# Decode state updates on row tiles of 32: two sequences in one product, two heads in two banks

## The chip, the cores and the metric

The kernel runs on one NeuronCore of a Trainium2 chip. The metric is the device time of one execution in microseconds (us); smaller is better. The engines are named as the profile names them: PE is the matrix engine and PEld its weight loads, DVE the vector engine, ACT the scalar engine, POOL the GpSimd engine, SP the engine that issues nearly all DMAs.

## What is computed

One decoder layer for 1024 prompt tokens and 8 decode sequences of 4 new tokens each (32 tokens). Two groups of four heads mix the tokens: an mLSTM (group a) and an HGRN2 (group b). Then come an output projection and a SwiGLU feed-forward layer. What matters here is the recurrent state of the decode sequences: each of the 8 sequences has a 128 x 128 matrix per head and group.

```python
# mLSTM, for each head:  num = w_inter * (q @ C) + (s_qk @ v)
C_new = decay[..., None, None] * C + jnp.einsum('bhs,bhsk,bhsv->bhkv', w_last, k, v)
n_new = decay[..., None] * n + jnp.einsum('bhs,bhsk->bhk', w_last, k)
...
# HGRN2, for each head:  inter = (q * exp(b)) @ S
S_new = jnp.exp(bL[:, :, 0, :])[..., None] * S + jnp.einsum('bhsk,bhsv->bhkv', k * jnp.exp(bL - b), v)
```

For a decode sequence the sums over s have four terms. The old state is needed twice: it is multiplied with the queries, and it is decayed and added to the new outer products.

## The kernel before

**Units and hooks.** The program is a list of units. A unit (`emit_k`, from L124) is one 128-row weight tile times a block of tokens: eight steps of the contraction, in each of them three products (L135 high weights by high activations, L136, L137), all into one PSUM bank of the tag `mm`. After every second step, and after the unit's evacuation, `hook()` (L63) is called: four hooks in a unit. Everything else is written as Python generators in a list `active`. A hook lets each of them write out its next instructions, in the order in which they were started; `yield n` means "go on n hooks later". So a hook is a place in the program order of all engines. Each engine works through its own instructions strictly in that order. `finish(key)` calls hooks until a generator is done, with no unit products in between.

**The token mixers.** The units come in the order: four heads of group a, each for three blocks of tokens (288, 384 and 384 wide, block 0 holding the 32 decode tokens), then four heads of group b in the same way. For group a the units of a block are q, k, v, o. The evacuation of a q or k unit (`conv_evac`, L404) writes out at once a chain of convolution steps on DVE (L435 to L445), a tanh on ACT (L449) and a last DVE step (L450). The prompt's mixing is `mix_a` (L506) and `mix_b` (L745), which take one to three banks of the tag `mx` at a time. There are four `mx` banks.

**The decode sequences.** `sample_a` (L700) and `sample_b` (L899) both go through `sample_core` (L600). The four heads' 32 tokens each lie on the 128 partitions: head h on partitions 32h to 32h+31.

- The keys are transposed (L612) and scaled into `ktm` (L619 to L624): a tile of [128, 4, 128] in which head h's block has its keys on its own 32 partitions and zeros elsewhere. The zeros come from a POOL memset in the first `mix_a` (L536). The values go to `vt` (L618).
- `prep(s)` (L628) makes for sequence s the queries with the other sequences' columns zeroed (`qz`, POOL) and the values with the other sequences' rows zeroed (`vm`, one DVE instruction, L634). In group a it also copies n into column 128 of the state tile.
- The loop over s (L667) multiplies queries with the old state: four products, one for each head, on column tiles of 32 (L672), into one bank `so` in which all sequences are summed.
- `update(s, vm)` (L639): four products `ktm[:, h, :]` by `vm`, each with the full 128 rows, into two `mx` banks (L644); one hook later four DVE instructions decay and add (L649), then the state is stored (L650).
- The state tiles `st` (L606) have two buffers, and `fetch(s + 2)` stands behind the store of s.

In group a the update of s directly follows its query products, and `prep(s + 1)` stands ahead of both; a sequence takes four hooks. In group b the loop does only the query products, every two hooks; a second generator `updates()` (L654), started at its end, fetches the states again and updates them, seven hooks for each sequence, with three hooks between `vm` (L660) and the products.

**Float32 products** appear in the trace as two passes: one `matmul` call with plain float32 operands gives two LDWEIGHTS and two MATMUL rows, so that the 32 calls of L644 in a group show as 64 rows. The unit products use a one-pass type and show one row each.

**What the driver forces.** `finish(("sa",))` stands four units into group b (L1791), `start(sample_b())` at the unit 12 x 3 + 8 of group b (L1793), and `finish(("su",))`, which waits for `updates()`, in the feed-forward part (L1816).

Of the kernel before, what the change touches and what calls it, by code (L numbers as in the profile page):

```python
# [24 lines left out]
H = 4  # L25
# [3 lines left out]
NS = 5  # L29
# [11 lines left out]
def hybrid_step(ctx: ExitStack, tc: tile.TileContext, i, o):  # L41
# [156 lines left out]
    def norm_rstd(key, n, acc, w=(2, 3)):  # L198
        """the rstd of n tokens on all partitions, from the squares summed over the feature tiles in acc"""
# [18 lines left out]
    def norm_gen(key, x, hv, lv, acc, vg, w=(2, 3), pb=None, lo_dve=(0, 4), step=2):  # L218
        """x = hv + lv = x * rstd * g, rstd from the squares summed over the feature tiles in acc"""
# [17 lines left out]
    # ------------------------------------------------------------------ token mixers  # L237
# [3 lines left out]
    # per-feature constants  # L241
# [26 lines left out]
    # ---- mLSTM gates  # L268
# [127 lines left out]
    # ---- mLSTM  # L396
# [57 lines left out]
    def early(name, h, b):  # L454
        if (name, h, b) == ("v", 0, 0):
            return ktm.rearrange("p h t -> p (h t)")
        if name != "q" or h or b == 2:
            return None
        return mp.tile([128, 4, 130], F32, tag="st", name="st", bufs=2).rearrange("p a c -> p (a c)")
# [30 lines left out]
    def norm_cols(s, sqs, nch, d2=None, p=128):  # L490
        """s = (sqs / 128 + EPS * d2) ** -0.5"""
# [14 lines left out]
    def mix_a(h, b):  # L506
# [28 lines left out]
        if (h, b) == (0, 0):  # L535
            nc.gpsimd.memset(ktm, 0.0)  # L536
# [63 lines left out]
    def sample_core(h_off, w, vnorm, st_in, decay, out_state, n_io, d2, k_scale, later=None):  # L600
        """the decode sequences of one head group: four heads x 32 tokens on the partitions"""
# [3 lines left out]
        def fetch(s):  # L605
            st = mp.tile([128, 4, 130], F32, tag="st", name="st", bufs=2)  # L606
            sts[s] = st
            nc.sync.dma_start(st[:, :, 0:128], st_in[s].rearrange("h k v -> k h v"))
        fetch(0)
        fetch(1)  # L610
# [8 lines left out]
        for h in range(H):  # L619
            hs = slice(32 * h, 32 * h + 32)  # L620
            if k_scale is None:
                nc.vector.tensor_copy(ktm[hs, h, :], pK[hs, 0:128])
            else:
                nc.vector.tensor_scalar_mul(ktm[hs, h, :], pK[hs, 0:128], k_scale[hs])  # L624
        pO = bank("so")
        vms, qzs = {}, {}

        def prep(s):  # L628
            st = sts[s]
            vm = vms[s] = mp.tile([128, 130], F32, tag="svm", name="svm", bufs=2)  # L630
            qz = qzs[s] = mp.tile([128, 4, 32], F32, tag="qz", name="qz", bufs=2)
            nc.gpsimd.memset(qz, 0.0)
            nc.gpsimd.tensor_copy(qz[:, :, 4 * s:4 * s + 4], qS[:, :, 4 * s:4 * s + 4])
            nc.vector.tensor_scalar_mul(vm[:, 0:w], vt[:, 0:w], seqm[:, s:s + 1])  # L634
            if w == 129:
                nc.gpsimd.tensor_copy(st[:, :, 128:129], n_io[0][:, 4 * s:4 * s + 4, None])
        prep(0)
        yield 3
        def update(s, vm):  # L639
            st = sts[s]  # L640
            pUs = [bank(), bank()]
            for h in range(H):
                u0 = (h % 2) * 130
                nc.tensor.matmul(pUs[h // 2][:, u0:u0 + w], ktm[:, h, :], vm[:, 0:w], start=True, stop=True)  # L644
            yield 1
            for h in range(H):
                u0 = (h % 2) * 130
                x = st[:, h, 0:w]
                nc.vector.scalar_tensor_tensor(x, x, decay(h, s), pUs[h // 2][:, u0:u0 + w], op0=OP.mult, op1=OP.add)  # L649
            nc.sync.dma_start(out_state[s].rearrange("h k v -> k h v"), st[:, :, 0:128])  # L650
            if w == 129:
                nc.gpsimd.tensor_copy(n_io[1][:, 4 * s:4 * s + 4, None], st[:, :, 128:129])

        def updates():  # L654
            fetch(0)
            fetch(1)
            yield 2
            for s in range(SEQS):
                vm = mp.tile([128, 130], F32, tag="svm", name="svm", bufs=2)
                nc.vector.tensor_scalar_mul(vm[:, 0:w], vt[:, 0:w], seqm[:, s:s + 1])  # L660
                yield 3
                yield from update(s, vm)
                if s + 2 < SEQS:
                    fetch(s + 2)
                yield 3

        for s in range(SEQS):  # L667
            if s + 1 < SEQS:
                prep(s + 1)
            st, qz = sts[s], qzs[s]  # L670
            for h in range(H):
                nc.tensor.matmul(pO[32 * h:32 * h + 32, 0:w], qz[:, h, :], st[:, h, 0:w], start=(s == 0), stop=False,  # L672
                                 skip_group_check=True, tile_position=(0, 32 * h))
# [54 lines left out]
    # ---- HGRN2  # L728
# [16 lines left out]
    def mix_b(h, b):  # L745
# [4 lines left out]
        samp = b == 0  # L750
        gx = tl("wib", 388, 2)
# [27 lines left out]
        while lv < 128:  # L779
# [123 lines left out]
    # ------------------------------------------------------------------ unit list  # L903
# [37 lines left out]
    # output projection; the token order from here on: 1024 prompt tokens, 32 decode tokens  # L941
# [62 lines left out]
    # feed-forward, first NPLAIN feature tiles  # L1004
# [36 lines left out]
    # feed-forward, the other feature tiles: pairs of them (rows of A) times two halves of the tokens (columns of B), the  # L1041
    # contraction in two halves: the seven products of Strassen and Winograd
# [21 lines left out]
    def t_prep():  # L1064
        """T1 = B12 - B11, T2 = B22 - T1, T3 = B22 - B12, T4 = B21 - T2"""
# [71 lines left out]
    def gsplit(g, u, dve=False):  # L1137
        """the factors of the products: A11 A12 | S1 = A21 + A22, S2 = S1 - A11 | S3 = A11 - A21, A22 | S4 = A12 - S2"""
# [52 lines left out]
    def g_out(u, r, th, j, ps, other=None, op=None):  # L1191
        """row tile r, token half th, columns j: ps or ps + other is there"""
# [54 lines left out]
    # down projection: NS times four feature tiles in the same way (the contraction in two pairs of tiles, pairs of output  # L1247
    # tiles, halves of the tokens), the last two tiles plainly
# [3 lines left out]
    def memb(r):  # L1252
        """place r of the ring of operands: hi and lo of two feature tiles, half of the tokens"""
# [18 lines left out]
    def raw_ff(c, f):  # L1272
        """the two column blocks of a feature tile: halves of the tokens, in the last chunk halves of each half"""
# [16 lines left out]
    def stage1(c):  # L1290
        """B11, T1 = B12 - B11, T2 = B22 - T1, B21"""
# [26 lines left out]
    def diffs(c, k):  # L1318
        """T3 = B22 - B12, T4 = B21 - B11 - T3"""
# [7 lines left out]
    def stage2(c):  # L1327
        """B22, T3, T4"""
# [28 lines left out]
    def dsplit(g):  # L1357
        """A11 A12 A22 | S1 = A21 + A22, S2 = S1 - A11, S4 = A12 - S2, S3 = A11 - A21"""
# [5 lines left out]
        def pair(j):  # L1364
            # the weights of the last chunk stay: five tiles in the ring, three in free places of the other ring
# [49 lines left out]
    def d_step(g, p):  # L1415
        """a product for a pair of output tiles, halves of the tokens; in the last chunk for two pairs, the quarters of a half"""
# [27 lines left out]
    # the first NPLAIN feature tiles of the down projection plainly  # L1444
# [36 lines left out]
    # the final norm: the first half of the tokens, then two quarters  # L1481
# [432 lines left out]
```

## Time and profile before

| | us |
|---|---|
| median of 3 runs | 1456.2 |
| lowest and highest run | 1451.91, 1456.57 |
| span of the profiled execution | 1451.2 |
| PE busy in it | 1376.6 |
| DVE busy in it | 904.0 |

The span is the time from the first to the last instruction of one profiled execution; it lies 5.0 us below the median of the runs and 0.7 us below the lowest of them. Rows of the timeline begin with the start and the duration in us; "x8" says that eight instructions were merged into the row, and brackets tell how long the engine had been idle and which instruction ended that. A matmul's start is recorded, its end is modelled, so the distance between starts is the safer measure of what a matmul costs.

### The profile page before, as it was taken

To read this page: it belongs to the slowest core of one execution; us is meant where nothing else is said; L and a number is where in the kernel's file an instruction comes from. 1 tells how busy PE (TensorE), PEld (TensorE's weight loads), DVE (VectorE), ACT (ScalarE), POOL (GpSimd) and SP (SyncE) were. 2 spreads that over 40 slices of the span, in tenths; PEclk is the share of its full clock that TensorE was granted. 3 is DMA by queue.
4 is the path that set the end of the run, shared out by engine and by line. 5 is a ranking of instruction groups with operands and counts; after the bars stand their busy time and mean duration, and the time that the engine had idled before them with its cause. 6 is when DMAs were issued, how large, how long until landed. Compare 5 with 4: busy or idle time off the path is not lost. (4 is left out here: it accounts for less than half of the span.)

```text
span 1451.2 us, 26916 instructions
## 1 busy us (share of the span) xinstructions
PE 1376.6 (95%) x10384; PEld 1339.6 (92%) x10384; DVE 904.0 (62%) x2120; ACT 528.8 (36%) x1195; POOL 731.9 (50%) x720
## 2 busy tenths in 40 slices
PE   7879999999999999999989999999999999998886
PEld 7769999999999998899989999999999998888885
DVE  7876657666776767745472233233322389999986
ACT  6554433322222223223344343333334423333343
POOL 5313213234343435223456655656555778888854
PEclk9989999999999999999999999999999999999998
DMA  6012212320010114443542222222212563334303
GB/s 216 22 42 76 64 37 86 109 79 29 33 44 18 44 32 133 142 148 119 182 139 74 82 89 89 69 72 89 89 64 69 182 235 134 134 134 145 123 30 121
DMA packets 85833, 138.54 MB, mean 95 GB/s; under 512 B 8240, under 2 KB 61000, under 8 KB 85192
## 3 DMA queue, kind: packets, MB, share of 16 engines
q1 hardware_dynamic: 85272, 136.57, 28.7%
q8 instruction: 82, 1.34, 0.4%
q14 instruction: 47, 0.39, 0.1%
q10 hardware_dynamic: 432, 0.24, 0.1%
HBM read 107.03 MB, written 29.75 MB: 94 GB/s over the span
## 5 line engine op out<-in xcount | busy, mean ns | idle before, releaser
L135 PE MATMUL mm<-HI,whi 128*128 128x384 f32 (+2 forms) x1160 | 382.7, 330 | 6.9 <-ACT gA L302 2.9
L137 PE MATMUL mm<-HI,wlo 128*128 128x384 f32 (+2 forms) x1160 | 363.8, 314 | 1.3 <-POOL wlo L97 1.3
L136 PE MATMUL mm<-LO,whi 128*128 128x384 f32 (+2 forms) x1160 | 363.9, 314 | 0.7 <-DVE LO L961 0.4
L135 PEld LDWEIGHTS mm<-HI,whi 128*128 128x128 f32 x1160 | 222.2, 192 | 12.2 <-ACT gA L302 3.2
L136 PEld LDWEIGHTS mm<-LO,whi 128*128 128x128 f32 x1160 | 222.4, 192 | 1.7 <-DVE LO L961 0.6
L137 PEld LDWEIGHTS mm<-HI,wlo 128*128 128x128 f32 x1160 | 221.9, 191 | 1.8 <-POOL wlo L97 1.8
L97 POOL TENSOR_TENSOR wlo<-raw,whi 128x512 fp32r<-128x512 f32 x90 | 119.7, 1339 | 144.1 <-ACT whi L96 99.2
L1158 POOL TENSOR_TENSOR wlo<-S,whi 128x512 fp32r<-128x512 f32 x78 | 107.0, 1373 | 87.1 <-ACT whi L1157 85.8
L1229 PE MATMUL mx<-T,whi 128*128 128x264 f32 x640 | 118.2, 284 | 0.0
L1229 PEld LDWEIGHTS mx<-T,whi 128*128 128x128 f32 x640 | 99.0, 188 | 0.0
L802 POOL TENSOR_TENSOR ck<-ck,wib 128x192 f32<-128x192 f32 (+2 forms) x72 | 41.2, 572 | 100.6 <-PE mx L757 56.2
L1229 PE MATMUL mx<-HI,whi 128*128 128x264 f32 x320 | 91.0, 284 | 0.0
L1229 PE MATMUL mx<-T,wlo 128*128 128x264 f32 x320 | 90.9, 284 | 0.0
L1229 PE MATMUL mx<-HI,wlo 128*128 128x264 f32 x320 | 90.9, 284 | 0.0
L1229 PE MATMUL mx<-LO,whi 128*128 128x264 f32 x320 | 90.7, 283 | 0.0
L1282 POOL TENSOR_TENSOR LO<-rg,HI 128x528 fp32r<-128x528 f32 x52 | 78.4, 1514 | 10.5 <-ACT HI L1281 5.8
L1435 PE MATMUL mx<-HI,whi 128*128 128x264 f32 x208 | 62.3, 300 | 9.9 <-DVE X L1439 9.9
L1157 ACT ACTIVATE whi<-S 128x512 fp32r<-128x512 f32 x80 | 50.2, 629 | 58.4 <-DVE S L1146 58.4
L1229 PE MATMUL mm<-HI,wlo 128*128 128x264 f32 x240 | 68.2, 284 | 0.0
L1229 PE MATMUL mm<-HI,whi 128*128 128x264 f32 x240 | 68.2, 284 | 0.0
L1229 PE MATMUL mm<-LO,whi 128*128 128x264 f32 x240 | 67.9, 283 | 0.0
L1439 DVE TENSOR_TENSOR X<-X,mx 128x264 f32<-128x264 f32 x160 | 60.7, 418 | 8.2 <-PE mx L1435 8.2
(544 smaller groups left out, 3751.8 us busy)
## 6 DMA issues: line engine op xcount, KB each, us to landing
rg<-d_ff SPq DMA_DIRECT2D x42, 528.0 KB
raw<-in_wA SPq DMA_DIRECT2D x31, 512.0 KB
raw<-in_wgu SPq DMA_DIRECT2D x24, 512.0 KB
raw<-in_wd SPq DMA_DIRECT2D x22, 512.0 KB
d_ff<-sg SPq DMA_DIRECT2D x40, 264.0 KB
rg<-in_wgu SPq DMA_DIRECT2D x20, 512.0 KB
d_h<-X SPq DMA_DIRECT2D x4, 1056.0 KB
X<-d_x SPq DMA_DIRECT2D x4, 1056.0 KB
```

The lines of the kernel that those rows point to most:

```text
L97: (nc.gpsimd if pool else nc.vector).tensor_tensor(lo[:, s], raw[:, s], hi[:, s].bitcast(F32), op=OP.subtract)
L135: nc.tensor.matmul(ps[:, :n], wh, rh[:, k, :], start=(k == 0), stop=False)
L136: nc.tensor.matmul(ps[:, :n], wh, rl[:, k, :], start=False, stop=False)
L137: nc.tensor.matmul(ps[:, :n], wl, rh[:, k, :], start=False, stop=(k == nk - 1))
L802: nc.gpsimd.tensor_tensor(ke, ke, gv[:, :, 1:2].to_broadcast([128, nb, lv]), op=OP.mult)
L1157: nc.scalar.activation(hi[:, s], t, AF.Copy)
L1158: (nc.vector if dve else nc.gpsimd).tensor_tensor(lo[:, s], t, hi[:, s].bitcast(F32), op=OP.subtract)
L1229: nc.tensor.matmul(ps[:, :QN], a[:, w], b_[:, kk, c], start=new and kk == 0 and x == 0, stop=kk == 3 and x == 2, skip_group_check=True)
L1282: (nc.vector if dve else nc.gpsimd).tensor_tensor(lw, src, h.bitcast(F32), op=OP.subtract)
L1435: nc.tensor.matmul(ps[:, :QN], a[:, w], b_[k][:, cs], start=new and k == 0 and x == 0, stop=k == 1 and x == 2, skip_group_check=True)
L1439: nc.vector.tensor_tensor(y, y, ps[:, :QN], op=OP.add)
```

## The change

1. The key tile is no longer padded: only `ktm[:, 0, :]` is used, with all heads' keys on their own partitions, written by one DVE instruction instead of four. The POOL memset goes.
2. `update(s)` handles two sequences. It writes two `vm` instructions into one tile, then, one hook later, the products of heads 0 and 1, one hook later their DVE steps, one hook later the products of heads 2 and 3, one hook later their DVE steps, one hook later both stores. A product takes 32 rows (`tile_position=(32 * h, 0)`) and both sequences' values side by side (2 x 129 or 2 x 128 columns). Each of the two heads has a bank of its own.
3. The query products of two sequences stand together. `vm` is no longer made in `prep`, so that group b makes it once instead of twice.
4. `st` and `qz` have four buffers, four states are fetched ahead. A pair takes seven hooks in group a (four for each sequence before), four in group b's query loop (two for each before) and nine in `updates()` (seven for each before).
5. The wait for `sample_a` in `mix_b` moves to its first line. The scratch memory for DMAs is made smaller, which makes room for the buffers.

```diff
@@ mix_a
-        if (h, b) == (0, 0):
-            nc.gpsimd.memset(ktm, 0.0)
@@ sample_core
-            st = mp.tile([128, 4, 130], F32, tag="st", name="st", bufs=2)
+            st = mp.tile([128, 4, 130], F32, tag="st", name="st", bufs=4)
...
-        fetch(0)
-        fetch(1)
+        for s in range(4):
+            fetch(s)
...
-        for h in range(H):
-            hs = slice(32 * h, 32 * h + 32)
-            if k_scale is None:
-                nc.vector.tensor_copy(ktm[hs, h, :], pK[hs, 0:128])
-            else:
-                nc.vector.tensor_scalar_mul(ktm[hs, h, :], pK[hs, 0:128], k_scale[hs])
+        kt = ktm[:, 0, :]
+        if k_scale is None:
+            nc.vector.tensor_copy(kt, pK[:, 0:128])
+        else:
+            nc.vector.tensor_scalar_mul(kt, pK[:, 0:128], k_scale)
...
-            qz = qzs[s] = mp.tile([128, 4, 32], F32, tag="qz", name="qz", bufs=2)
+            qz = qzs[s] = mp.tile([128, 4, 32], F32, tag="qz", name="qz", bufs=4)
...
-            nc.vector.tensor_scalar_mul(vm[:, 0:w], vt[:, 0:w], seqm[:, s:s + 1])
...
         prep(0)
+        prep(1)
         yield 3
-        def update(s, vm):
-            st = sts[s]
-            pUs = [bank(), bank()]
-            for h in range(H):
-                u0 = (h % 2) * 130
-                nc.tensor.matmul(pUs[h // 2][:, u0:u0 + w], ktm[:, h, :], vm[:, 0:w], start=True, stop=True)
+        def update(s):
+            vm = mp.tile([128, 2, 130], F32, tag="svm", name="svm", bufs=2)
+            for j in range(2):
+                nc.vector.tensor_scalar_mul(vm[:, j, 0:w], vt[:, 0:w], seqm[:, s + j:s + j + 1])
             yield 1
-            for h in range(H):
-                u0 = (h % 2) * 130
-                x = st[:, h, 0:w]
-                nc.vector.scalar_tensor_tensor(x, x, decay(h, s), pUs[h // 2][:, u0:u0 + w], op0=OP.mult, op1=OP.add)
-            nc.sync.dma_start(out_state[s].rearrange("h k v -> k h v"), st[:, :, 0:128])
...
+            for hp in (0, 2):
+                pUs = [bank()[:, :260].rearrange("p (j k) -> p j k", k=130) for _ in range(2)]
+                for h in (hp, hp + 1):
+                    hs = slice(32 * h, 32 * h + 32)
+                    nc.tensor.matmul(pUs[h - hp][:, :, 0:w], kt[hs, :], vm[hs, :, 0:w], start=True, stop=True,
+                                     tile_position=(32 * h, 0))
+                yield 1
+                for j in range(2):
+                    for h in (hp, hp + 1):
+                        x = sts[s + j][:, h, 0:w]
+                        nc.vector.scalar_tensor_tensor(x, x, decay(h, s + j), pUs[h - hp][:, j, 0:w],
+                                                       op0=OP.mult, op1=OP.add)
+                yield 1
+            for j in range(2):
+                st = sts[s + j]
+                nc.sync.dma_start(out_state[s + j].rearrange("h k v -> k h v"), st[:, :, 0:128])
...
         def updates():
-            fetch(0)
-            fetch(1)
+            for s in range(4):
+                fetch(s)
             yield 2
-            for s in range(SEQS):
-                vm = mp.tile([128, 130], F32, tag="svm", name="svm", bufs=2)
-                nc.vector.tensor_scalar_mul(vm[:, 0:w], vt[:, 0:w], seqm[:, s:s + 1])
-                yield 3
-                yield from update(s, vm)
-                if s + 2 < SEQS:
-                    fetch(s + 2)
-                yield 3
+            for s in range(0, SEQS, 2):
+                yield from update(s)
+                for j in (4, 5):
+                    if s + j < SEQS:
+                        fetch(s + j)
+                yield 4
...
+        for s in range(0, SEQS, 2):
+            for j in (2, 3):
+                if s + j < SEQS:
+                    prep(s + j)
+            for j in range(2):
+                st, qz = sts[s + j], qzs[s + j]
+                for h in range(H):
+                    nc.tensor.matmul(pO[32 * h:32 * h + 32, 0:w], qz[:, h, :], st[:, h, 0:w], start=(s + j == 0), stop=False,
+                                     skip_group_check=True, tile_position=(0, 32 * h))
             if later is None:
-                yield from update(s, vms[s])
-            if s + 2 < SEQS:
-                fetch(s + 2)
-            yield 3 if later is None else 2
+                yield from update(s)
+            for j in (4, 5):
+                if s + j < SEQS:
+                    fetch(s + j)
+            yield 2 if later is None else 4
@@ mix_b
+        while samp and ("sa",) not in done:
+            yield 1
...
             if samp and lv == 2:
-                while ("sa",) not in done:
-                    yield 1
@@ kernel
-    nc = _bacc.Bacc("TRN2", target_bir_lowering=False, num_devices=1)
+    nc = _bacc.Bacc("TRN2", target_bir_lowering=False, num_devices=1, dynamic_dma_scratch_size=2048)
```

More of the change, by code (lines that the diff above doesn't have):

```diff
@@ L458, in early @@
             return None
-        return mp.tile([128, 4, 130], F32, tag="st", name="st", bufs=2).rearrange("p a c -> p (a c)")
+        return mp.tile([128, 4, 130], F32, tag="st", name="st", bufs=4).rearrange("p a c -> p (a c)")
     def act_evac(name, tag, func, bj, h, b, bufs=1, silu=False):
@@ L618, in sample_core @@
         nc.scalar.activation(vt[:, 0:128], pV[:, 0:128], AF.Copy)
[L619 to L624 removed]
+        kt = ktm[:, 0, :]
[3 more added lines that the diff above has]
+            nc.vector.tensor_scalar_mul(kt, pK[:, 0:128], k_scale)
         pO = bank("so")
[L626 removed]
+        qzs = {}
         def prep(s):
             st = sts[s]
[L630 to L631 removed]
+            qz = qzs[s] = mp.tile([128, 4, 32], F32, tag="qz", name="qz", bufs=4)
             nc.gpsimd.memset(qz, 0.0)
             nc.gpsimd.tensor_copy(qz[:, :, 4 * s:4 * s + 4], qS[:, :, 4 * s:4 * s + 4])
[L634 removed]
             if w == 129:
```

11 lines of the change are left out of this document (2 added, 9 removed).

## The prediction

> **What bounds the kernel now.** I read the busy times first, then the windows of the two stages in which the decode states are updated (246 to 302 us for group a; for group b 552 to 646 us, of which the window shows the first half), then the timeline of PE inside them. The columns of the windows are PE, PEld, DVE, ACT and POOL busy, each with its count of instructions, the granted clock, the DMA share and GB/s.
>
> ```profile
> PE 1376.6 (95%) x10384; PEld 1339.6 (92%) x10384; DVE 904.0 (62%) x2120; ACT 528.8 (36%) x1195; POOL 731.9 (50%) x720
> ```
>
> ```profile
> 246.00:302.00 56.00, 54.42 (x404) 50.78 (x403) 38.30 (x117) 19.06 (x45) 18.90 (x45) 1.00 0.39 119
> 552.00:600.00 48.00, 43.60 (x358) 38.08 (x357) 39.75 (x108) 18.41 (x44) 23.56 (x35) 0.96 0.57 171
> ```
>
> PE is the bound in both: it idles 1.6 and 4.4 us, and nothing else is nearly full. So a product saved on PE is time saved, and a wait put in PE's queue is time lost, whatever the other engines do. DVE is the engine to watch: at 68% and 83% busy, and in strict order, it can run some us behind PE's place in the program.
>
> **What the bursts on PE cost.** The distance between starts tells it. First a burst of query products in the unit stream, then one of update products.
>
> ```profile
> 575.40 0.33 PE L136 MATMUL mm<-LO,whi 128*128 128x384 f32 x1
> 575.57 0.34 PE L137 MATMUL mm<-HI,wlo 128*128 128x384 f32 x1
> 575.84 0.43 PE L672 MATMUL so<-st,qz 128*32 128x128 f32 x8
> 576.19 0.45 PE L135 MATMUL mm<-HI,whi 128*128 128x384 f32 x1
> 576.48 0.34 PE L136 MATMUL mm<-LO,whi 128*128 128x384 f32 x1
> ```
>
> ```profile
> 602.82 0.28 PE L136 MATMUL mm<-LO,whi 128*128 128x264 f32 x1
> 602.94 0.28 PE L137 MATMUL mm<-HI,wlo 128*128 128x264 f32 x1
> 603.06 1.05 PE L644 MATMUL mx<-svm,ktm 128*128 128x128 f32 x8
> 603.87 0.37 PE L135 MATMUL mm<-HI,whi 128*128 128x264 f32 x1
> 604.07 0.28 PE L136 MATMUL mm<-LO,whi 128*128 128x264 f32 x1
> ```
>
> A unit product takes 0.17 us (384 columns) or 0.12 us (264). From L137 to the second product after the burst: 0.91 less two intervals of 0.17 is **0.56 us** for a query burst, 1.13 less 0.24 is **0.89 us** for an update burst. The query burst pays about 0.1 us on entering and 0.1 us on leaving, the update burst nothing on entering (603.06 is one interval after 602.94).
>
> Two other bursts on column tiles give the rate inside one:
>
> ```profile
> 243.32 0.27 PE L714 MATMUL mx<-sq,sk 128*32 128x32 f32 x8
> 243.52 0.44 PE L135 MATMUL mm<-HI,whi 128*128 128x384 f32 x1
> ```
>
> ```profile
> 588.09 0.38 PE L788 MATMUL mx<-qw,ck 128*32 128x32 f32 x12
> 588.40 0.39 PE L135 MATMUL mm<-HI,whi 128*128 128x264 f32 x1
> ```
>
> L714 puts two passes of 32 columns on each of four tiles and takes 0.20; L672 two passes of 128 on each of four, 0.35; L788 six of 32 on each of two, 0.31. If tiles run beside each other, the busiest one streams 64, 256 and 192 columns, and 0.15 + 0.8 ns for each column fits all three (0.20, 0.35, 0.30). The update burst, 8 passes of 128 on the whole array, is 0.81, again 0.8 ns a column.
>
> **The change, part by part.**
>
> *Query products of two sequences together.* The second eight passes add 256 columns on each tile, 0.21 us, in place of a burst of 0.56: 0.35 less for each of 8 pairs, **-2.8 us**.
>
> *Update products.* Before, 16 bursts of 0.89 (14.2 us). After, also 16 bursts, of four passes: two heads on two row tiles, 258 columns. No row shows row tiles of 32 beside each other, so both ends: beside each other, the busiest tile streams 516 columns, 0.41, and the burst is 0.56 - 0.21 + 0.41 = 0.76; one after the other, 1032 columns, 1.18. The weights are wider than in L672, and a load of 32 rows is not shorter for its few rows:
>
> ```profile
> L672 PEld LDWEIGHTS so<-st,qz x128: 106/109/155, 252.1 to 583.4; 128*32 128x32 f32 x128
> ```
>
> ```profile
> L1658 PEld LDWEIGHTS mx<-ident,nrs 32*128 32x128 f32 x1 | 0.2, 179 | 0.3 <-issue 0.3
> ```
>
> I add the 0.08 us between them for the first load and take 0.85, next to L672, the only kind of tile that the trace shows: 16 x 0.04, **-0.6 us**; ends -2.1 (0.76) and +5.9 (1.26).
>
> [...]
>
> *One key instruction, no early `vm`.* Two PE waits stand behind DVE instructions (L557 and L806, in the brackets) that queue behind work which the change shortens, and one behind POOL's `qz`:
>
> ```profile
> 249.54 1.43 DVE L624 TENSOR_SCALAR ktm<-mx,scol 32x128 f32<-32x128 f32 x4
> 251.01 0.32 DVE L634 TENSOR_SCALAR svm<-svt,cst 128x129 f32<-128x129 f32 x1
> ```
>
> ```profile
> 251.71 0.49 PE L572 MATMUL mx<-C,qw 128*128 128x129 f32 x2 [1.58 <-DVE C L557]
> ```
>
> ```profile
> 552.27 1.19 DVE L622 COPY ktm<-mx 32x128 f32<-32x128 f32 x4
> 553.49 0.57 DVE L634 TENSOR_SCALAR svm<-svt,cst 128x128 f32<-128x128 f32 x1
> ```
>
> ```profile
> 557.87 0.43 PE L788 MATMUL mx<-qw,ck 128*32 128x32 f32 x12 [1.96 <-DVE wib L806]
> ```
>
> ```profile
> 583.40 0.43 PE L672 MATMUL so<-st,qz 128*32 128x128 f32 x8 [0.43 <-POOL qz L633]
> ```
>
> In group a three of four key instructions (1.1) and the `vm` (0.3) go: 1.4 of 1.58. In group b 0.9 and 0.57: about 1.4 of 1.96. `qz` is then made four hooks ahead instead of two: 0.4. Together **-3.2 us**.
>
> *The wait that comes.* `vm` used to stand a whole sequence (group a) or three hooks (group b) ahead of the products that need it; now it is one hook. PE stands still at the product until DVE has got that far, and the unit products queued behind it wait too, and all their evacuations. How far DVE lags:
>
> ```profile
> 252.13 0.43 PE L672 MATMUL so<-st,qz 128*32 128x129 f32 x8
> ```
>
> ```profile
> 255.34 0.28 DVE L634 TENSOR_SCALAR svm<-svt,cst 128x129 f32<-128x129 f32 x1
> ...
> 286.83 0.56 DVE L450 SCALAR_TENSOR_TENSOR ck<-raw,ck 128x384 f32<-128x384 f32 x1 [0.66 <-ACT raw L449]
> ...
> 287.50 0.86 DVE L583 TENSOR_SCALAR kt<-mx,sm 128x128 f32<-128x128 f32 x3
> ```
>
> ```profile
> 282.95 0.58 ACT L416 ACTIVATE raw<-mm,vec 128x384 f32<-128x384 f32 x1 [1.38 <-PE mm L137]
> ```
>
> Pair 0 of group a starts at the hook of 252.13. `vm` comes behind the q unit's convolution, at 255.34, and two take 0.5: 255.85. PE gets to the update after 0.77 (0.56 + 0.21) of queries and a hook of six products (1.04), at 253.95: it waits 1.9 us. Counting the yields, pairs 1 and 2 fall at the ends of units without a convolution just before (0.1 each, an estimate), and pair 3 at the second hook after the k unit that ends at 282.9: there DVE is free at 288.3 (behind L450 and L583), `vm` done at 288.8, PE ready at 282.9 + 2.1 + 0.77 + 1.04 = 286.8: 2.0. Together **+4.1**. In group b:
>
> ```profile
> 613.84 0.42 DVE L978 TENSOR_TENSOR X<-X,mm 128x264 f32<-128x264 f32 x1
> 614.81 0.43 DVE L984 TENSOR_TENSOR raw<-raw,nt 128x264 f32<-128x264 f32 x1 [0.55 <-ACT nt L980]
> 615.16 0.28 DVE L660 TENSOR_SCALAR svm<-svt,cst 128x128 f32<-128x128 f32 x1
> ```
>
> A `vm` behind a unit's evacuation (pair 1 by the count) comes 1.3 us after L978 and is done at 1.85, a hook is 0.73: it waits 1.1. Pair 2, a hook later, 0.4; the others none: **+1.5**.
>
> *Banks.* Heads 2 and 3 take two more `mx` banks two hooks after heads 0 and 1, while the mixers hold some. In pair 2 of group a one of them is a bank whose DVE steps stand behind the next q convolution:
>
> ```profile
> 275.98 0.58 ACT L416 ACTIVATE raw<-mm,vec 128x384 f32<-128x384 f32 x1 [5.76 <-PE mm L137]
> ```
>
> ```profile
> 280.41 1.12 DVE L649 SCALAR_TENSOR_TENSOR st<-st,wiS,mx 128x129 f32<-128x129 f32 x4
> ```
>
> Its third DVE step ends at 281.3; PE is there at 275.9 + 0.85 + 2.1 + 1.1 (the mixer's products) = 279.9. That is 1.4, and about 0.6 each at two other places where `mix_a` or `mix_b` holds three banks (an estimate, from DVE steps of 0.3 to 0.6). Which bank is given isn't in the trace: between 0 and 2.6, I take half, **+1.3**.
>
> *What costs nothing.* Transfers keep their number. SP's queue has the fetch behind a store in both kernels:
>
> ```profile
> SPq L608 <- DMA out_Cs<-st: 13.0, 6, 2.8
> ```
>
> Six such waits in group a become two, each behind two stores; the weight loads queued behind them are two tiles ahead. The moved wait in `mix_b` falls on nothing: `sample_a` needs 38 hooks instead of 41, and the first `mix_b` starts 40 hooks after it. The POOL memset stood ahead of no PE wait.
>
> **Sum.** -2.8 - 0.6 - 3.2 + 4.1 + 1.5 + 1.3 = +0.3 us on the profiled execution's span of 1451.2. That execution lies 5.0 us below the median of the runs (0.7 below the lowest), so on the median: **1456.5 us**. A measurement of this kernel can tell about 0.3% (4.4 us) from no change.
>
> **The rivals.**
>
> *Faster: the waits don't come.* If DVE, freed of fourteen instructions (three key steps in each group, eight `vm` in group b), keeps up with PE, the gains alone remain: -6.6, 1449.6 us. For it: DVE has 30% free in the stage. Against: the convolution chain is serial with ACT and stands ahead of `vm` in DVE's order however free DVE is. Chance 0.25.
>
> *Slower: row tiles don't run beside each other*, the change then not doing what its tile positions say. Price: bursts of 1.26 instead of 0.85, 16 x 0.41 = +6.6, 1463.1 us. It decides from a burst above 0.89. For it: no row shows row tiles. Against: column tiles do run beside each other. Chance 0.12.
>
> *Slower: `vm` late in all pairs of group a and every bank wait in full*: +3.6 +1.3, 1461.4 us; it decides if the hooks fall otherwise than I count. Chance 0.13.
>
> *Forecast*, within 0.3%: chance 0.5, its own range 1452 to 1460.5. So faster 0.25, same 0.5, slower 0.25; the range from 1450 to 1463 leaves out about half of each outer case.
>
> **What the profile will show.** Right: update bursts of 0.75 to 0.9 us with four passes and 258 columns; 16 query passes in about 0.56; L572 and L788 with waits under 0.5; PE waits of about 2 us for `svm` in pairs 0 and 3 of group a. Wrong: update bursts over 1.1, or no PE wait for `svm` at all, or new waits far from 246 to 302 and 552 to 646 us.

## The result and the profile after

| | before | after |
|---|---|---|
| median, us | 1454.16 (4 runs) | 1471.71 (4 runs) |
| lowest and highest run | 1451.91, 1456.57 | 1465.64, 1475.09 |
| span of the profiled execution | 1451.2 | 1473.3 |

The changed kernel is slower: the ratio of the times is 1.0114, interval 1.009 to 1.0138. That is 17.6 us on the medians and 22.1 us between the two profiled executions. The time lies above the range of the prediction. (The kernel before has a fourth run here, 1452.13 us, beside the three that the prediction started from.)

From here on line numbers are those of the changed kernel: the update products are L646 (L644 before), their DVE steps L652 (L649), `vm` L640 (L634, L660), the query products L679 (L672), the key instruction L621, the state fetch L606 (L606), and the two products with old waits L570 (L572) and L798 (L788).

The page's busy row of the changed kernel:

```profile
PE 1387.9 (94%) x10320; PEld 1344.1 (91%) x10320; DVE 899.6 (61%) x2106; ACT 528.5 (36%) x1195; POOL 729.8 (50%) x719
```

PE executes 64 instructions fewer than before and is yet busy 11.3 us longer. Work that was taken away cannot do that; the same work took longer. The windows of the two stages say how (columns as before: PE, PEld, DVE, ACT, POOL busy, granted clock, DMA share, GB/s; group b's window is moved by the 12 us that the program is late by then):

```profile
246.00:302.00 56.00, 49.18 (x307) 41.44 (x307) 35.04 (x107) 15.48 (x40) 14.95 (x41) 0.92 0.31 90
...
564.00:612.00 48.00, 43.51 (x362) 39.52 (x361) 38.69 (x107) 18.52 (x44) 23.22 (x36) 0.96 0.62 179
```

In group a PE got through 307 products where it had done 404 (32 of the 97 are missing only because two update products became one), idles 6.8 us instead of 1.6, and its clock is 0.92 instead of 1.00. There are two losses, idle time and clock. The idle time first, in the view of waits for PE, from 240 to 330 us and from 540 to 660 us (total us, times, longest):

```profile
PE mx L646 <- DVE svm L640: 3.2, 1, 3.2
PE mx L646 <- DVE sm L577: 3.2, 1, 3.2
PE mx L702 <- DVE sjunk L699: 0.8, 1, 0.8
PE mx L646 <- DVE st L652: 0.4, 1, 0.4
...
PE mx L646 <- DVE svm L640: 3.8, 2, 2.1
PE mx L646 <- DVE st L652: 2.1, 1, 2.1
PE mx L803 <- POOL ck L812: 1.0, 1, 1.0
PE mx L798 <- DVE wib L816: 1.0, 1, 1.0
```

The update products now wait for `svm` four times, 3.2, 3.2, and 3.8 for two. (The row that names `sm` L577 is a `vm` too. L577 is the next instruction on DVE, from 256.63 to 256.78, and the product doesn't read its result; the two `vm` end at 256.72, below, and the product starts at 256.86.) One more stop, 2.1, stands behind a DVE step L652. The wait of L572 (1.58 before) is gone, that of L788 is 1.0 instead of 1.96.

Now the clock, behind the first of these stops. The windows of the changed kernel, two microseconds each, for PE alone (busy, count, granted clock, DMA share, GB/s); the product that waited starts at 256.86:

```profile
254.00:256.00 2.00, 0.00 (x0) 1.00 0.68 263
256.00:258.00 2.00, 1.14 (x7) 1.00 0.49 171
258.00:260.00 2.00, 2.00 (x10) 0.69 0.03 8
260.00:262.00 2.00, 2.00 (x8) 0.50 0.00 0
262.00:264.00 2.00, 2.00 (x7) 0.50 0.00 0
264.00:266.00 2.00, 2.00 (x9) 0.60 0.00 0
266.00:268.00 2.00, 2.00 (x16) 1.00 0.48 139
```

PE is full again from 258 on, but it gets through 7 to 9 products in two microseconds where it does 16 at the end: the clock is at half. The missing share, (0.31 + 0.50 + 0.50 + 0.40) x 2 us = 3.4 us, is time lost on top of the 3.17 us of the stop. "Clock lost" below means this sum over a stretch, (1 - clock) x time. From 240 to 330 us it is 0.0 before and 6.8 after; from 540 to 660 us, 1.7 and 6.8. Ahead of 240 us it is 10.2 and 11.9, from 660 us to the end of each span 16.5 and 20.2. So 1.7 and 3.7 us of loss were added outside the two stages as well; in the kernels of the experiments the first of these stretches loses between 10.2 and 15.4 us.

The same could have been read in the kernel before, behind its own stop of 1.96 us at 557.87:

```profile
556.00:558.00 2.00, 0.13 (x9) 1.00 0.71 243
558.00:560.00 2.00, 2.00 (x18) 0.52 0.00 0
560.00:562.00 2.00, 2.00 (x14) 0.63 0.68 196
```

(0.48 + 0.37) x 2 = 1.7 us of clock, behind a stop that the prediction priced at 1.96.

The products themselves came out as predicted. The timeline of PE, a query burst of two sequences and an update burst:

```profile
267.62 0.34 PE L137 MATMUL mm<-HI,wlo 128*128 128x384 f32 x1
267.89 0.65 PE L679 MATMUL so<-st,qz 128*32 128x129 f32 x16
268.46 0.44 PE L135 MATMUL mm<-HI,whi 128*128 128x384 f32 x1
268.74 0.33 PE L136 MATMUL mm<-LO,whi 128*128 128x384 f32 x1
...
269.45 0.34 PE L137 MATMUL mm<-HI,wlo 128*128 128x384 f32 x1
269.72 0.70 PE L646 MATMUL mx<-svm,ktm 32*128 32x258 f32 x4
270.35 0.44 PE L135 MATMUL mm<-HI,whi 128*128 128x384 f32 x1
270.63 0.34 PE L136 MATMUL mm<-LO,whi 128*128 128x384 f32 x1
```

From L137 to the second product behind the burst: 1.12 for the queries, 1.18 for the update. Less two unit intervals of 0.17 that is 0.77 and **0.83**. So the row tiles do run beside each other. They also pay about 0.1 us on entering (0.27 from L137 to the burst, where a unit product takes 0.17) and 0.1 on leaving, as the column tiles do.

Two update bursts of group a took longer at full clock:

```profile
274.18 1.42 PE L646 MATMUL mx<-svm,ktm 32*128 32x258 f32 x4
275.53 0.44 PE L135 MATMUL mm<-HI,whi 128*128 128x384 f32 x1
...
286.71 0.70 PE L646 MATMUL mx<-svm,ktm 32*128 32x258 f32 x2
287.77 0.67 PE L646 MATMUL mx<-svm,ktm 32*128 32x258 f32 x2 [0.36 <-DVE st L652]
288.37 0.44 PE L135 MATMUL mm<-HI,whi 128*128 128x384 f32 x1
```

From their first start to the next unit product they took 1.35 and 1.66 us, where the burst at 269.72 took 0.63. In the burst at 269.72 the four passes start two and two, 0.01 us apart; in these two bursts they start one after the other, 0.3 us and more apart. That is what a second bank that comes late would do; the bracket of 287.77 names the DVE step that empties a bank, for 274.18 no row names a cause. The loss is 0.72 and 1.03, 1.75 us together, of which the view of waits shows only 0.36, because it counts from the modelled end of a product.

### Why the two stops in group a are longer than worked out

The timeline of DVE and POOL in the changed kernel, ahead of the two stops that end at 256.86 and 297.88:

```profile
251.57 1.27 POOL L97 TENSOR_TENSOR wlo<-raw,whi 128x512 fp32r<-128x512 f32 x1
251.62 1.39 DVE L435 COPY raw<-hist 128x3 f32<-128x3 f32 x1
...
256.24 0.48 DVE L640 TENSOR_SCALAR svm<-svt,cst 128x129 f32<-128x129 f32 x2
...
295.17 2.48 POOL L97 TENSOR_TENSOR wlo<-raw,whi 128x512 fp32r<-128x512 f32 x2 [2.48 <-ACT whi L96]
295.85 1.88 DVE L640 TENSOR_SCALAR svm<-svt,cst 128x129 f32<-128x129 f32 x2
```

A copy of three columns (median 0.16 us) takes 1.39 and ends at 253.01, just behind POOL's L97, which ends at 252.84. Two `vm` take 1.88 instead of 0.48 and end at 297.73, behind the second of two L97, at 297.65. The excess is 1.2 and 1.4 us, nearly all by which the stops were mis-sized (3.17 for 1.9, 3.21 for 2.0). The timeline of the kernel before has the same pair:

```profile
283.04 1.29 POOL L97 TENSOR_TENSOR wlo<-raw,whi 128x512 fp32r<-128x512 f32 x1
283.57 0.92 DVE L439 COPY cvo<-raw 128x3 f32<-128x3 f32 x1 [1.35 <-ACT raw L416]
```

Again a copy of three columns ends (284.49) when L97 does (284.33). Not every DVE instruction beside an L97 is longer: three L581, which read a product from PSUM, take 0.86 together beside the L97 of 295.17, and the 32 of them in the changed kernel take 0.34 to 0.35 each. No run was made for this part: three DVE instructions end 0.08 to 0.17 us behind a POOL instruction, and that the POOL instruction held them is argued from that and not shown.

### The profile page after: what moved, and what is told of

It reads as the page before. It is cut to its first block, busy times and chain, and to the rows that moved or that the text cites. A ratio compares the mean times of both kernels' runs of the same rounds, so it can differ in the third digit from the quotient of the medians.

```text
span 1473.3 us, 26771 instructions
## 1 busy us (share of the span) xinstructions
PE 1387.9 (94%) x10320; PEld 1344.1 (91%) x10320; DVE 899.6 (61%) x2106; ACT 528.5 (36%) x1195; POOL 729.8 (50%) x719
## 5 line engine op out<-in xcount | busy, mean ns | idle before, releaser
L135 PE MATMUL mm<-HI,whi 128*128 128x384 f32 (+2 forms) x1160 | 387.1, 334 | 5.0 <-ACT st L417 1.8
L137 PE MATMUL mm<-HI,wlo 128*128 128x384 f32 (+2 forms) x1160 | 367.8, 317 | 1.3 <-POOL wlo L97 1.3
L136 PE MATMUL mm<-LO,whi 128*128 128x384 f32 (+2 forms) x1160 | 367.8, 317 | 0.4 <-POOL LO L225 0.2
L135 PEld LDWEIGHTS mm<-HI,whi 128*128 128x128 f32 x1160 | 225.7, 195 | 16.4 <-issue 8.1
L136 PEld LDWEIGHTS mm<-LO,whi 128*128 128x128 f32 x1160 | 226.0, 195 | 1.3 <-POOL LO L225 0.5
L137 PEld LDWEIGHTS mm<-HI,wlo 128*128 128x128 f32 x1160 | 225.3, 194 | 1.8 <-POOL wlo L97 1.8
L97 POOL TENSOR_TENSOR wlo<-raw,whi 128x512 fp32r<-128x512 f32 x90 | 119.1, 1332 | 156.6 <-ACT whi L96 110.8
L1237 PE MATMUL mx<-T,whi 128*128 128x264 f32 x640 | 118.2, 284 | 0.0
L1237 PEld LDWEIGHTS mx<-T,whi 128*128 128x128 f32 x640 | 99.0, 188 | 0.0
L1237 PE MATMUL mx<-HI,whi 128*128 128x264 f32 x320 | 91.0, 284 | 0.0
L1237 PE MATMUL mx<-T,wlo 128*128 128x264 f32 x320 | 90.9, 284 | 0.0
L1237 PE MATMUL mx<-HI,wlo 128*128 128x264 f32 x320 | 90.9, 284 | 0.0
L1237 PE MATMUL mx<-LO,whi 128*128 128x264 f32 x320 | 90.7, 283 | 0.0
L1237 PE MATMUL mm<-HI,wlo 128*128 128x264 f32 x240 | 68.2, 284 | 0.0
L1237 PE MATMUL mm<-HI,whi 128*128 128x264 f32 x240 | 68.2, 284 | 0.0
L1237 PE MATMUL mm<-LO,whi 128*128 128x264 f32 x240 | 67.9, 283 | 0.0
```

Source lines behind the costliest of these rows:

```text
L97: (nc.gpsimd if pool else nc.vector).tensor_tensor(lo[:, s], raw[:, s], hi[:, s].bitcast(F32), op=OP.subtract)
L135: nc.tensor.matmul(ps[:, :n], wh, rh[:, k, :], start=(k == 0), stop=False)
L136: nc.tensor.matmul(ps[:, :n], wh, rl[:, k, :], start=False, stop=False)
L137: nc.tensor.matmul(ps[:, :n], wl, rh[:, k, :], start=False, stop=(k == nk - 1))
L1237: nc.tensor.matmul(ps[:, :QN], a[:, w], b_[:, kk, c], start=new and kk == 0 and x == 0, stop=kk == 3 and x == 2, skip_group_check=True)
```

## The experiments

Theory: the time goes into PE stops for `vm` (and one for a state fetch), each worth its length plus the clock behind it; the row tiles and the merged bursts are a small gain. Rivals: the row tiles or the paired banks themselves cost the time; or the clock is low for a reason that has nothing to do with the stops. All ratios are to runs of the kernel before on the same chip, whose median was 1454.6 beside experiments 1, 2, 3 and 5 (one chip) and 1454.9 beside 4, 6, 7 and 8 (another). Differences to the changed kernel are between medians that were not taken side by side; beside it, the kernel before had 1454.16.

**1. `vm` two sequences early, all else as in the change.**

```diff
+        def mkvm(s):
+            if s >= SEQS:
+                return
+            vm = vms[s] = mp.tile([128, 2, 130], F32, tag="svm", name="svm", bufs=2)
+            for j in range(2):
+                nc.vector.tensor_scalar_mul(vm[:, j, 0:w], vt[:, 0:w], seqm[:, s + j:s + j + 1])
...
@@ update
-            vm = mp.tile([128, 2, 130], F32, tag="svm", name="svm", bufs=2)
-            for j in range(2):
-                nc.vector.tensor_scalar_mul(vm[:, j, 0:w], vt[:, 0:w], seqm[:, s + j:s + j + 1])
+            vm = vms[s]
...
+                if hp:
+                    mkvm(s + 2)
```

`mkvm(0)` stands behind `prep(1)` in group a and at the start of `updates()` in group b.

> The changed kernel with one thing moved: the masked values vm of a pair are written on DVE right behind the products of heads 2 and 3 of the pair before (of the first pair: with the first queries' preparation, or with the fetches), some four hooks ahead of their products instead of one. Products, banks, transfers and hooks stay. Theory 'waits' (PE stands still for vm, and the granted clock then falls to 0.5 for about 7 us after each stop of 2 us or more): the four stops of 1.7 to 3.2 us and the low clock behind them go, 10 us of waiting and 10 to 14 us of lost clock less in the profile, time 1451 to 1457 us; the wait for a late state fetch in group b (2.1 us) stays. Theory 'products' (the row tiles, the banks or the denser transfers cost the time): 1467 to 1474 us, as the changed kernel.

Measured: 1453.01 us, ratio 0.9986 (0.9972 to 1.0); 18.7 us less than the changed kernel. No wait for `svm` is left, and the clock lost is 0.0 and 1.7. What remains from 540 to 660 us is the stop behind the state fetch:

```profile
PE mx L653 <- DVE st L661: 2.4, 1, 2.4
```

So the stops and their clock made all of the loss; row tiles, pairs of banks and merged bursts are still in this kernel.

**2. The kernel before, with `vm` only one hook ahead.** The reverse: none of the change but the late `vm`.

```diff
-        def update(s, vm):
+        def update(s):
             st = sts[s]
+            vm = mp.tile([128, 130], F32, tag="svm", name="svm", bufs=2)
+            nc.vector.tensor_scalar_mul(vm[:, 0:w], vt[:, 0:w], seqm[:, s:s + 1])
+            yield 1
```

The `vm` in `prep` and in `updates()` goes, and the loops yield one hook less for each sequence, so that the hooks' number stays the same.

> The kernel before with only this: vm of each sequence is written one hook ahead of its products (in group a in the same hook as the queries, products one hook later; in group b one hook instead of three), the same number of hooks for each sequence. Full-array products, padded keys, two states ahead, as before. Theory 'waits': stops of 1 to 3 us in four or five sequences of group a and one to three of group b, most with the low clock behind them: 1462 to 1478 us. Theory 'products': 1452 to 1458 us, no change.

Measured: 1467.28 us, ratio 1.0078 (1.0049 to 1.0107). Its waits from 240 to 330 us:

```profile
PE mx L645 <- DVE svm L640: 5.1, 3, 2.5
PE mx L645 <- DVE sm L579: 2.0, 1, 2.0
```

Four stops for `vm` (the row with `sm` is one, as above), 7.1 us, and 3.4 us of clock; two more in group b, 1.6 together. That is 12.1 us, beside 12.7 between the medians and 10.8 between the profiled executions. One hook is too short for `vm` on its own, without row tiles.

**3 and 4. Stops of chosen length in the kernel before.** A small product is followed by n ACT copies into its bank and a second small product, so that PE must wait for ACT. The cut shows experiment 4; in experiment 3 the first product was missing, and ACT ran ahead of PE.

```diff
+        if ui in PROBE:
+            pw = bank("so")
+            nc.tensor.matmul(pw[:, 0:1], ident, ones, start=True, stop=True)
+            for _ in range(PROBE[ui]):
+                nc.scalar.activation(pw, ones[:, 0:1].to_broadcast([128, 512]), AF.Copy)
+            nc.tensor.matmul(pw[:, 0:1], ident, ones, start=True, stop=True)
         emit_unit(u)
```

> The kernel before with four stops of PE put into group b's second and third head, 40 us apart: ahead of one unit each stands a small product that waits for 1, 2, 3 and 5 copies on ACT (512 columns, about 0.6 us each, behind the evacuation of the unit before). The products are extra work and change no output. PE stops of about 1.5, 2.2, 2.8 and 4 us. Theory 'a stop also costs clock': behind the stops of 2 us or more the granted clock is 0.5 for about 7 us, so these units take some 3.4 us more each: +10.5 of waiting +10 of clock, about 1475 us. Theory 'a stop costs its own length': clock 1.0 throughout, +10.5, about 1465 us.

Measured: 1461.56 us, ratio 1.0048 (1.0027 to 1.0069). The four stops were 0, 1.5, 0.56 and 3.4 us, not the lengths that were meant, so the expectation missed. Only the longest was followed by a low clock (1.7 us lost).

> The kernel before with eight stops of PE in group b, four units (some 28 us) apart: a small product, 1, 2, 3 or 4 copies on ACT that wait for it (0.6 us each), and a second small product that waits for the copies; the eight are 1, 2, 3, 4, 1, 2, 3, 4 copies. Extra work, no output changes. Stops of about 0.9, 1.5, 2.1 and 2.7 us, 14.4 in all. Theory 'a stop also costs clock from about 1.7 us on': none behind 0.9, seldom behind 1.5, mostly behind 2.1 and 2.7, in portions of 1.7 us (a stretch of 3.4 us at half clock): 14 + 3 to 10 us over the kernel before. Theory 'only long stops cost clock' (3 us and more): 14 us and clock 1.0 at all eight.

Measured: 1477.45 us, ratio 1.0164 (1.0126 to 1.0203; two runs), 22.5 us more than the kernel before. The eight stops add up to 15.0 us (longest 3.0), and in four places 1.7 us of clock is lost, 6.8 in all: 21.8. Of the eight, neither of two near 0.9 (0.74 and 1.12) lowered the clock, one of two near 1.5 did (1.53, not 1.75), both near 2.1 did, and one of two between 2.6 and 3.0 (3.02, not 2.64). So stops do make the low clock, which the second rival denied, but length alone does not decide it.

What else tells the stops apart can be read from the traces. In each of the ten profiled executions the granted clock changes, from its first change to its last, only at times that lie a whole number of 3.41 us apart. These times cut an execution into windows. Three stops of this run, by these windows, with the window's length and PE's busy time first (2.16 us that end at 420.36, 2.64 that end at 449.01, 1.53 that end at 498.25):

```profile
417.38:420.79 3.41, 1.25 (x12) 1.00 0.01 2
420.79:424.20 3.41, 3.41 (x12) 0.50 0.00 0
...
444.68:448.10 3.42, 1.68 (x15) 1.00 0.00 0
448.10:451.51 3.41, 2.50 (x27) 1.00 0.00 0
451.51:454.92 3.41, 3.41 (x28) 1.00 0.00 0
...
495.88:499.30 3.42, 1.89 (x16) 1.00 0.00 0
499.30:502.71 3.41, 3.41 (x22) 0.50 0.00 0
```

The stop of 2.16 lies whole in one window, and the next window is low. The stop of 2.64 falls on a border, 1.74 and 0.91, and no window is low. From 240 to 660 us of all ten executions, 24 low stretches begin, each right behind a window in which PE stood still for 1.50 us or more, and each is one window or two long (3.41 or 6.83 us). Behind windows with 1.83 us or more of it the clock fell in 16 of 16 cases, with 1.50 to 1.74 in 8 of 15, with 1.40 or less in none. That is a count in these traces and not a rule: near 700 us a window with 1.13 us (694.60, kernel before) and one with 1.17 (712.74, changed kernel) were followed by a low one too, and what makes a low stretch last one window or two was not found.

**5. Experiment 1, and three more hooks between the state fetches of `updates()` and its first `vm`.**

```diff
                 fetch(s)
-            yield 2
+            yield 5
```

> As the run before, and the first update of group b comes three hooks later behind its fetches (yield 5 instead of 2). Theory 'waits': the stop of 2.1 us and its low clock go too, 4 to 6 us under the run before, 1446 to 1452 us, faster than both kernels. Theory 'products': no difference to the run before.

Measured: 1446.8 us, ratio **0.9942** (0.9915 to 0.9969): faster than both kernels. The view of waits from 540 to 660 us has only short ones left, no clock is lost in either stage:

```profile
PE mx L813 <- POOL ck L822: 1.0, 1, 1.0
PE mx L808 <- DVE wib L826: 1.0, 1, 1.0
```

So with both waits gone the change is a gain. Its terms, from the kernel before: bursts -2.8 (queries) and -1.0 (updates, 16 x 0.06), L572's wait -1.2 (0.4 is left here), L788's -1.0 and its clock -1.7, `qz` -0.4, and +3.6 for four update bursts that took 1.35 to 1.66 us instead of 0.63, as above; together -4.5. The two stages got 4.2 us shorter, all of it in group b (197.7 to 193.5); group a takes 108.1 us in both kernels. The profiled executions are 5.4 apart, the medians 7.8: the rest of the medians' difference is not in these two traces. The late second banks are a cost that is still in this kernel.

What the stop was that the three hooks removed, in the changed kernel's timeline (SPq is SP's queue of DMA issues):

```profile
599.60 2.10 SPq L606 DMA_DIRECT2D st<-in_S  x4
...
604.72 0.61 DVE L652 SCALAR_TENSOR_TENSOR st<-st,gS,mx 128x128 f32<-128x128 f32 x2 [1.30 <-DMA st<-in_S]
...
606.06 0.92 PE L646 MATMUL mx<-svm,ktm 32*128 32x256 f32 x4 [2.08 <-DVE st L652]
```

DVE waits for the first state, and PE for the bank that this DVE step empties. Four fetches are issued together here, two in the kernel before; experiment 5 shows that three hooks are enough, not which of the two made the state late.

**6. Experiment 5 without row tiles.** Padded keys again (four DVE instructions and the memset), products with 128 rows, still two sequences in one product and two banks.

```diff
-                    nc.tensor.matmul(pUs[h - hp][:, :, 0:w], kt[hs, :], vm[hs, :, 0:w], start=True, stop=True,
-                                     tile_position=(32 * h, 0))
+                    nc.tensor.matmul(pUs[h - hp][:, :, 0:w], ktm[:, h, :], vm[:, :, 0:w], start=True, stop=True)
```

> The run with early vm and the later first update, with the row tiles undone: keys padded again (four DVE instructions, POOL memset), products of 128 rows, still two sequences side by side and two heads in two banks. Update bursts of four passes on one array: 4 x 258 x 0.8 ns, 0.83 inside and about 0.9 with both ends, against 0.83 with row tiles. Theory 'the row tiles are worth little': +1 us for the bursts and +1 to 2 for stops behind the three more DVE instructions in each group: 1447 to 1451 us. Theory 'the row tiles are the gain': 1453 us or more.

Measured: 1453.69 us, ratio 0.9995 (0.9979 to 1.001), 6.9 above experiment 5 (6.6 if each is taken from its own runs of the kernel before). That is above what was expected, and in the range given for the row tiles being the gain. The bursts are hardly dearer (0.87 for 0.83, 16 x 0.04 = 0.6 us). What came back are two waits behind DVE:

```profile
PE mx L572 <- DVE C L557: 2.2, 1, 2.2
...
PE mx L809 <- DVE wib L827: 2.6, 2, 1.6
```

L572 is 1.8 longer than in experiment 5 and 1.7 of clock follow it; L809's line is 1.6 longer. Three bursts whose second bank is late cost 1.9 instead of 3.6. With the 0.6 that is 4.0, and the two stages are 4.0 longer. Another 2.0 of the 6.1 between the profiled executions lies ahead of them (244.6 for 242.6 us), where experiment 1 took 245.3; it is not explained. So by these traces the row tiles are worth little on PE itself; the one key instruction that they allow is worth more, on DVE. The key instructions alone were not varied.

**7 and 8. `vm` early in one group alone.** As experiment 1, with `mkvm` for group a only, then for group b only.

```diff
-                if hp:
+                if hp and later is None:
                     mkvm(s + 2)
```

(`later is not None` in the other.)

> The changed kernel with vm early in group a only. Theory 'waits': two stops of 3.2 us and two low stretches worth 3.4 us go: 13 us under the changed kernel, 1456 to 1461 us, and group b keeps its stops. Theory 'products': as the changed kernel.

Measured: 1462.31 us, ratio 1.0041 (1.0018 to 1.0065), 9.4 less than the changed kernel and just above what was expected; single runs lie between 1453.1 and 1465.3. Group b keeps its stops (3.8 and 2.2 us), and in the profiled execution, one of the longer ones, 10.2 us of clock is lost there, where the changed kernel lost 6.8 behind the same stops. The runs differ as their clocks do: the four shortest (up to 1457.8) had a mean granted clock of 0.976 to 0.983, the six others 0.971 to 0.975.

> The changed kernel with vm early in group b's updates only (first update not later). Theory 'waits': two stops (1.7 and 2.1 us) and low stretches worth 5 us go, the wait for the state fetch stays: 6 to 9 us under the changed kernel, 1461 to 1467 us. Theory 'products': as the changed kernel.

Measured: 1462.68 us, ratio 1.0068 (1.0042 to 1.0094), 9.0 less than the changed kernel. Group a keeps its two stops of 3.2, with 5.1 us of clock instead of 6.8. The two parts, 9.4 and 9.0, add up to 18.4, near the 18.7 of experiment 1.

Clock lost in the two stages, one profiled execution each, and in the whole execution, (1 - mean clock) x span, as the mean of all runs (their number in brackets; this includes low clock at places where PE stands still anyway):

| us | 240 to 330 | 540 to 660 | whole, all runs |
|---|---|---|---|
| before | 0.0 | 1.7 | 29.5 (21), 31.3 (19) |
| after | 6.8 | 6.8 | 40.8 (4) |
| 1, `vm` early | 0.0 | 1.7 | 30.2 (10) |
| 5, and later after the fetches | 0.0 | 0.0 | 28.3 (5) |
| 2, before with `vm` late | 3.4 | 1.7 | 33.7 (5) |
| 6, as 5, without row tiles | 1.7 | 0.0 | 28.7 (10) |
| 7, early in group a | 0.0 | 10.2 | 35.2 (10) |
| 8, early in group b | 5.1 | 1.7 | 38.8 (4) |

So the clock that the change lost is no accident of one execution: over all runs it is 9.5 or 11.3 us, by which of the two sets of runs of the kernel before one takes.

## Why the prediction was wrong

Its terms, in its order, against the two profiled executions:

| term | predicted | shown |
|---|---|---|
| query products of two sequences together | -2.8 | -2.8 |
| update products | -0.6 | -1.0 |
| waits that go (L572, L788, `qz`) | -3.2 | -3.0 |
| waits for `vm`, group a | +4.1 | +6.4 |
| waits for `vm`, group b | +1.5 | +3.8 |
| banks | +1.3 | +1.8 |
| "What costs nothing": the state fetch | 0 | +2.1 |
| clock lost behind stops | no term | +11.9 |
| sum | +0.3 | +19.2 |

The starts of rows that both timelines have give the same from another side. From the first L714 (243.3; L722 after, 244.5) to the first L894 (351.5; L902 after, 364.1) group a's stage took 108.1 us and takes 119.5: +11.4. From the key transposes of group b (L612, 548.4; L610 after, 561.0) to the first L1229 (746.1; L1237 after, 765.1) it was 197.7 and is 204.1: +6.4. Together that is 17.8, where the terms have 19.2. For group a they have 11.5, beside 11.4. For group b they have 7.7, beside 6.4: three short waits of the kernel before (L757, L136 and L135, 1.0 in all) are 0.3 in the changed one, and the last 0.6 isn't explained. The other 4.3 us of the 22.1 lie outside, 1.2 ahead of 243 us and 3.1 behind 746 us. The clock lost rose there by a little more, from 10.2 to 12.0 and from 14.8 to 18.5. This execution was the longest of the four and had the lowest mean clock, 0.969 (0.973 to 0.974 in the others); the medians are 17.6 apart.

1. **The step that failed is the first: "a wait put in PE's queue is time lost"**, priced at the wait's own length, wherever it was used. Here a stop of 1.7 us or more usually took 1.7 or 3.4 us of clock with it. That is 11.9 of the 17.5 by which the two stages came out longer than the sum (17.8 for 0.3). The window of 552 to 600 us, quoted in the prediction, had the clue in it: its clock of 0.96 is 0.04 x 48 = 1.9 us, nearly all behind the stop of 1.96.
2. **"The wait that comes"** was right in kind and place: pairs 0 and 3 of group a, 1 and 2 of group b. It was mis-sized: 3.17 and 3.21 for 1.9 and 2.0, where by the timelines DVE's own instructions are 1.2 and 1.4 us longer beside POOL's L97; 1.70 and 2.09 for 1.1 and 0.4 in group b, where the lag was counted from a single unit of the kernel before.
3. **"Transfers keep their number"**, at no cost, failed once. Their number stayed, but the first DVE step now comes four hooks behind the fetches instead of six (2 + 1 + 1 for 2 + 3 + 1), and waited for DMA: 2.08 us on PE.
4. **The bursts** held: 0.77 and 0.83 for 0.77 and 0.85, so the rival "row tiles don't run beside each other" (1.26) fell. Experiment 6 adds that the whole array would have taken 0.87 here.
5. **The waits that go** held (1.58 to none, 1.96 to 0.99, `qz` to none), and the banks came near the middle that was taken (1.75 of up to 2.6, for 1.3).
6. **The faster rival**, 1449.6 if the waits don't come, is about what experiment 5 shows: -7.8 us on the medians where the rival said -6.6. The nearness is in part luck. The rival counted neither the 1.7 us of clock that go with L788's wait nor any late bank, and these cost 3.6 there. The slower rival with `vm` late in all pairs priced its stops too low for the same reason as the forecast.

## What to carry to other kernels

Here stops of 1.53 to 3.21 us had 1.7 or 3.4 us of lost clock behind them in most cases, and none in others (2.64, 1.97, 1.75, 1.58). So when PE is the bound, give a stop of such a length two prices, its length alone and its length plus the clock, and look in the kernel before for what the clock does behind its stops. The ten runs of experiment 7 lie between 1453.1 and 1465.3 us, with mean clocks of 0.971 to 0.983, so take several runs before you believe either price. An instruction of an engine that lags should be written out as early as its inputs and buffers allow: one `vm` two sequences ahead turned this change from 1.1% slower to 0.6% faster, together with three hooks between fetch and use. A merged, cheaper product saves little by itself (3.8 us here) and can cost as much by the banks that it needs (3.6 in experiment 5), so compare waits before and after, not only bursts.

## What was not expected of the hardware

- Behind a stop of PE the granted clock fell to 0.50 for about 3.4 or 6.8 us, at a cost of 1.7 or 3.4 us. Stops of 1.53, 1.70, 1.96, 2.08, 2.09, 2.16, 3.17 and 3.21 us have it behind them; stops of 2.64, 1.97 (experiment 2) and 1.75, L572's 1.58 in the kernel before and the two near 0.9 of experiment 4 do not.
- In the ten profiled executions the clock changed on a grid of 3.41 us. From 240 to 660 us it was low behind 16 of 16 windows in which PE stood still for 1.83 us or more, 8 of 15 with 1.50 to 1.74, and none with 1.40 or less; near 700 us it was low behind windows with 1.13 and 1.17.
- With the clock at half PE looks busy: PE's busy time rose by 11.3 us with 64 instructions fewer. The count of products in a window shows it (8 for 16).
- A DVE copy of three columns took 1.39 us instead of 0.16; it ended 0.17 us behind a POOL instruction of 1.27 us that had begun 0.05 us ahead of it.
